# Seven plain pairs, token forms dealt one step per pair, plain tokens in idle tiles

## The chip, the core and the metric

The kernel runs on one core of a Trainium2 chip. Its engines work side by side, each through its own queue in order: TensorE (PE, with weight loads listed as PEld) multiplies, VectorE (DVE) and ScalarE (ACT) work elementwise, GpSimd (POOL) too, and SyncE (SP) issues most transfers. The metric is the device time of one execution in microseconds; lower is better.

## The reference

A two-layer decoder trunk on 512 tokens of width 1024. Layer 0 mixes tokens with retention and mLSTM heads, layer 1 with sparse attention. After each mixer comes the feed-forward block that this change touches, and then a gated per-layer embedding:

```python
def conv_ffn(h, w_up, conv_w, conv_b, w_down):
    a, b = jnp.split(h @ w_up, 2, axis=-1)
    a = causal_dwconv(a, conv_w, conv_b)
    return (jax.nn.gelu(a) * b) @ w_down

h = h + conv_ffn(rms_norm(h, ffn_norm_g[i]), ffn_w_up[i], ...)
e = rms_norm(p[i] @ ple_w[i], ple_norm_g[i])
gate = jax.nn.sigmoid(rms_norm(h, ple_gate_norm_g[i]) @ ple_w_gate[i])
h = h + gate * e
```

w_up is 1024 x 5632, w_down 2816 x 1024, the convolution is causal over three tokens, all in float32.

## The kernel before

**Precision.** Each float32 operand is split into a rounded part (hi) and a remainder (lo); a product is three matmuls, hi x hi, hi x lo and lo x hi (`mm3`, lines 176 to 178). A weight block is loaded into a raw tile `wr`, ACT writes the rounded part `wh` (L136), DVE the remainder `wl` (L137). The pool `wp` has three buffers of each.

**The feed-forward stage** (`ffn`) keeps tokens in columns: h is eight tiles of 128 x 512. `norm_in` makes the plain tokens, hi and lo of each of the eight h tiles times the norm's gain (L244, L245), in 16 of the 22 `g` tiles. The hidden width 2816 is 22 blocks f of 128. Block f needs a pair: a(f) from one half of w_up and b(f) from the other.

- Blocks below `PLAIN` (6) are **plain pairs** (`mm_up`): two products of a 128-row weight block with the tokens, 2 x 8 x 3 matmuls of 512 columns. `act_up` (L1386 to L1389) then scales by the norm (`rb`), convolves (L1374 to L1376), applies gelu (L1377), scales again on POOL (L1388), multiplies by b and keeps hi and lo as `gt[f]` in two g tiles.
- The others are **spread pairs** (`up`): the pair is seen as a 2 x 2 block product and done in seven products instead of eight, each on half the tokens: 4 x 3 matmuls of 256 columns. They need sums of weight blocks (class `Weights`: raw tiles `one` in wr, `two` in an `ep` slot by f modulo 4, and `es`; split parts fh/fl, gh/gl, eh/el, one buffer each) and sums of token halves, the **token forms** (`forms`), four steps of seven y tiles each. ACT copies a bank between two products that share it (L1447).

`down` (a job) multiplies the kept blocks of a part of the hidden width (`PARTS`) with two row blocks of w_down and adds to h (L1479). One job is named in each round of the loop; the first part, three blocks, is named in rounds 3 to 6. `e.early(m)` reads a tile of the embedding back from DRAM, squares it (L232) and adds it up on DVE (L234), one tile in each of rounds 1 to 8, the norm in round 9.

**What sets the order.** The program names instructions in loop order; a planner then gives each engine its sequence ahead of time, from a model of durations, from data dependencies and from free buffers. `high_priority(offset=AHEAD)` lets weight loads and splits go 500 places ahead of their place in the program. `behind(engine)` ties what a block issues on an engine behind the last instruction named there before the block. PSUM has four banks `a`, three `b` and one `o`; a plain pair takes one a and one b, a down job two b.

The round before the change:

```python
if f == 1:
    self.forms(n, C_FFN + 8 * i)
if jobs:
    down(*jobs.pop(0))
e.early(f - 1)
```

Of the kernel before, what the change touches and what calls it, by code (L numbers as in the profile page):

```python
# [11 lines left out]
F32 = mybir.dt.float32  # L12
F32R = mybir.dt.float32r
# [7 lines left out]
P = 128  # L21
T = 512
NTT = T // P
D = 1024
KD = D // P
# [14 lines left out]
UNITS = ((3, (0,)), (3, (1,)), (2, (0,)), (2, (1,)), (1, (0, 1)), (0, (0, 1)))  # L40
BANKS = {"a": 4, "b": 3, "o": 1}
AHEAD = 500
PLAIN = 6
H = T // 2

C_AB, C_NSA, C_FFN, C_PLE, C_PLG = 0, 8, 16, 32, 48
# [17 lines left out]
class Trunk:  # L64
# [73 lines left out]


    def load_late(self, src):  # L140
        raw = self.wp.tile([P, 1024], F32, name=self.nm("wr"), tag="wr")
        hi = self.wp.tile([P, 1024], F32R, name=self.nm("wh"), tag="wh")
        lo = self.wp.tile([P, 1024], F32R, name=self.nm("wl"), tag="wl")
        with self.tc.high_priority(offset=AHEAD):
            self.nc.sync.dma_start(raw, src)
        return (hi, lo), lambda: self.nc.scalar.activation(hi, raw, AF.Copy), lambda: self.nc.gpsimd.tensor_tensor(lo, raw, hi.bitcast(F32), ALU.subtract)

    def load(self, src, n=1024, cuts=1):

        nc = self.nc  # L150
        eng = {"v": nc.vector, "g": nc.gpsimd}[self.lo_seq[0]]
        self.lo_seq = self.lo_seq[1:] + self.lo_seq[0]
        raw = self.wp.tile([P, 1024], F32, name=self.nm("wr"), tag="wr")
        hi = self.wp.tile([P, 1024], F32R, name=self.nm("wh"), tag="wh")
        lo = self.wp.tile([P, 1024], F32R, name=self.nm("wl"), tag="wl")
        with self.tc.high_priority(offset=AHEAD):
            for c in range(cuts):
                s = slice(n // cuts * c, n // cuts * (c + 1))
                nc.sync.dma_start(raw[:, s], src[:, s])
                self.split(hi[:, s], lo[:, s], raw[:, s], eng)  # L160
        return hi, lo

    def load_parts(self, srcs, n):
        raw = self.wp.tile([P, 1024], F32, name=self.nm("wr"), tag="wr")
        hi = self.wp.tile([P, 1024], F32R, name=self.nm("wh"), tag="wh")
        lo = self.wp.tile([P, 1024], F32R, name=self.nm("wl"), tag="wl")
        w = slice(0, n * len(srcs))
        with self.tc.high_priority(offset=AHEAD):
            for x, src in enumerate(srcs):
                self.nc.sync.dma_start(raw[:, x * n : x * n + n], src)  # L170
            self.split(hi[:, w], lo[:, w], raw[:, w])
        return hi, lo
# [5 lines left out]
        mm(out, al, bh, start=False, stop=last, **kw)  # L178

    def packed(self, src):  # L180
        raw = self.wp.tile([P, 1024], F32, name=self.nm("wr"), tag="wr")
        w = self.wp.tile([P, 1024], F32R, name=self.nm("wh"), tag="wh").rearrange("p (k c m) -> p k c m", k=KD, c=2)
        r = raw[:, : KD * 64].rearrange("p (k m) -> p k m", k=KD)
        with self.tc.high_priority(offset=AHEAD):
            self.nc.sync.dma_start(raw[:, : KD * 64], src)
            self.split(w[:, :, 0], w[:, :, 1], r)
        return w
# [66 lines left out]

    def forms(self, n, c0):
        nc = self.nc
        minus = self.sc()
        nc.scalar.activation(minus, n.b, AF.Copy, scale=-1.0)
        sub = lambda out, a, b: nc.vector.tensor_tensor(out, a, b, ALU.subtract)
        neither = lambda out, a, b: nc.vector.scalar_tensor_tensor(out, a, -1.0, b, ALU.mult, ALU.subtract)  # L260
        n.f = []
        for k in range(KD // 2):
            x1, x2 = self.sc(), self.sc()
            for x, kk in ((x1, k), (x2, k + KD // 2)):
                nc.vector.scalar_tensor_tensor(x, self.h[kk], self.col(c0 + kk), minus, ALU.mult, ALU.mult)
            ta, tb = self.sc(), self.sc()
            b11, b12, b21, b22 = x1[:, :H], x1[:, H:], x2[:, :H], x2[:, H:]
            sub(ta[:, :H], b11, b12)
            neither(ta[:, H:], b22, ta[:, :H])
            sub(tb[:, :H], b22, b12)  # L270
            neither(tb[:, H:], b21, ta[:, H:])
            one = self.y()
            self.split(one[:, :H], one[:, H:], b11, nc.gpsimd)
            got = {1: (one[:, :H], one[:, H:])}
            for src, left, right in ((x2, 2, 3), (ta, 5, 6), (tb, 7, 4)):
                hi, lo = self.y(), self.y()
                self.split(hi, lo, src, nc.gpsimd if left == 2 else nc.vector)
                got[left], got[right] = (hi[:, :H], lo[:, :H]), (hi[:, H:], lo[:, H:])
            n.f.append(got)

    def norm_scale(self, n):
        self.norm_sum(n)
        self.norm_cast(n)
# [1069 lines left out]
    def ffn(self, i, e):  # L1353
        nc, I, tc = self.nc, self.I, self.tc
        with ExitStack() as ctx:
            fp = ctx.enter_context(tc.tile_pool(name=f"ffn{i}", bufs=1))

            def g_tile():
                return fp.tile([P, T], F32R, name=self.nm("g"), tag="g", bufs=22)

            n = self.norm_in(C_FFN + 8 * i, g_tile)
            gt = {}

            def mm_up(f):
                self.cycle = ("a", "b")
                return self.ws(I["w_up"][i, f], n), self.ws(I["w_up"][i, NF + f], n)
# [13 lines left out]
            def keep(f, c):  # L1380
                gt[f] = g_tile(), g_tile()
                self.split(*gt[f], c)
# [9 lines left out]
            class Weights:  # L1392
# [8 lines left out]

                def load(me):
                    f = me.f
                    me.one = self.wp.tile([P, 1024], F32, name=self.nm("wr"), tag="wr")
                    me.two = self.slot(f % 4).rearrange("p a t -> p (a t)")
                    nc.sync.dma_start(me.one, I["w_up"][i, f])
                    nc.sync.dma_start(me.two, I["w_up"][i, NF + f])
                    nc.gpsimd.dma_start(me.two[:, :T], me.two[:, T:], accum_op=ALU.add)  # L1408
# [14 lines left out]

            ahead = [Weights(PLAIN)]

# [10 lines left out]

            def product(ps, w, name, first):
                hi, lo = w[name]
                for k in range(KD // 2):
                    s = slice(k * P, k * P + P)  # L1440
                    self.mm3(ps, hi[:, s], lo[:, s], *n.f[k][name], first and k == 0, k == KD // 2 - 1, skip_group_check=True)

            def up(f):
                w = weights(f)
# [23 lines left out]
            def down(part, j):  # L1468
                f0, f1 = PARTS[part]
                w = (f1 - f0) * P  # L1470
                hi, lo = self.load_parts([I["w_down"][i, m, :, f0 * P : f1 * P] for m in (2 * j, 2 * j + 1)], w)
                self.cycle = ("b",)
                for b in range(2):
                    m = 2 * j + b
                    ps = self.bank()
                    for f in range(f0, f1):
                        s = slice(b * w + (f - f0) * P, b * w + (f - f0 + 1) * P)
                        self.mm3(ps, hi[:, s], lo[:, s], gt[f][0], gt[f][1], f == f0, f == f1 - 1)
                    nc.vector.tensor_tensor(self.h[m], self.h[m], ps, ALU.add)  # L1479

            self.lo_seq = "v"
            first = mm_up(0)
# [3 lines left out]
            for f in range(1, NF):  # L1486
                if f < PLAIN:
                    if f == PLAIN - 1:
                        with tc.high_priority(offset=AHEAD):
                            ahead[0].load()  # L1490
                            ahead[0].open()
                    act_up(f, *mm_up(f))
                else:
                    up(f)
                if f == 1:
                    self.forms(n, C_FFN + 8 * i)
                if jobs:
                    down(*jobs.pop(0))
                e.early(f - 1)
                for part, (f0, f1) in enumerate(PARTS):  # L1500
                    if f == f1 - 1:
                        jobs += [(part, j) for j in range(KD // 2)]
# [6 lines left out]
    class Embed:  # L1509
# [4 lines left out]
        def step(self, m):  # L1514
            if m == 0:
                self.inputs()
            if m % 4 == 0:
                self.w = self.k.load(self.k.I["w_ple"][self.i, m // 4])
            self.keep(m, self.products(m, self.w))
# [25 lines left out]

        def early(self, m):
            tr = self.k
            if m < KD:
                t = tr.sc()
                tr.nc.sync.dma_start(t, self.away[m * P : (m + 1) * P])  # L1550
                tr.acc_square(self.n, m, t, tr.nc.vector)
            elif m == KD:
                tr.norm_scale(self.n)
# [144 lines left out]
```

## Time and profile before

| | |
|---|---|
| time, median of 3 runs | 1365.17 us (1364.6 to 1366.2) |
| time of the profiled execution | 1365.49 us |
| its span | 1363.5 us |
| PE busy | 1338.6 us, 98% |
| DVE busy | 1007.2 us, 74% |
| ACT busy | 733.2 us, 54% |
| POOL busy | 415.3 us, 30% |
| mean granted PE clock | 0.994 |

The page cuts the span into 40 slices of 34 us and gives each engine's share of busy time in tenths. "The windows" give busy time and number of instructions for chosen stretches, with the granted clock of PE (1 is full), the DMA share and GB/s. A group's row gives line, engine, operation, tiles written and read, shape, count, busy us and mean ns, and after the second bar the idle time before it and what ended it. A row of the timeline gives start, duration, engine, line and tiles; brackets hold the idle time before it. A row of waits gives who waited for whom, us in total, times, and the longest.

### The profile page before, as it was taken

How to read it: one execution, taken by the hardware profiler on the slowest of the kernel's cores; microseconds unless marked ns; L12 is line 12 of the kernel's file. 1: busy time of each engine (PE TensorE's matmuls, PEld its weight loads, DVE VectorE, ACT ScalarE, POOL GpSimd, SP SyncE). 2: the span in 40 equal slices, each digit the busy share in tenths (PEclk: the TensorE clock that was granted, in tenths of full speed). 3: DMA queues.
4: the chain of work that ended last, by engine and by line, in shares of the span. 5: the costliest groups of instructions: out<-in, count | busy, mean ns of one | idle time of the engine just before them, and what ended most of it. 6: DMA issues, size and time to landing. Idle time of an engine off the chain costs nothing.

```text
span 1363.5 us, 21238 instructions
## 1 busy us (share of the span) xinstructions
PE 1338.6 (98%) x7854; PEld 1155.8 (85%) x7854; DVE 1007.2 (74%) x1644; ACT 733.2 (54%) x1313; POOL 415.3 (30%) x424
## 2 busy tenths in 40 slices
PE   9999999989999999999999999999989999999998
PEld 6888888768999999988788888887868999999987
DVE  5765866797777767687777878766797777767675
ACT  5357525454455445455366888674454455445452
POOL 3356422241111110330421887573240111110320
PEclk9999999989999999999999999999999999999999
DMA  6522348233555553423243331124233555553431
GB/s 221 157 99 93 109 139 247 89 105 109 156 160 153 166 140 101 155 97 116 95 156 110 105 94 51 32 82 126 80 101 116 158 154 158 158 146 95 155 101 70
DMA packets 69456, 168.82 MB, mean 124 GB/s; under 512 B 8164, under 2 KB 12900, under 8 KB 69352
## 3 DMA queue, kind: packets, MB, share of 16 engines
q1 hardware_dynamic: 59848, 150.55, 33.5%
q0 software_dynamic: 9216, 16.78, 7.5%
q8 instruction: 62, 1.02, 0.3%
q14 instruction: 42, 0.34, 0.1%
q10 hardware_dynamic: 288, 0.14, 0.0%
HBM read 147.76 MB, written 7.35 MB: 114 GB/s over the span
## 4 chain that ended last, share of the span: by engine, by line
PE 82%; DVE 9%; ACT 3%; issue 2%; DMA 2%; POOL 1%; SPq 0%; POOLq 0%; DVEq 0%; ACTq 0%
PE ps L176 23%; PE ps L177 23%; PE ps L178 23%; PE ps L1108 3%; PE ps L1083 2%; DVE wl L137 2%; PE ps L1052 1%; PE ps L1053 1%; ACT wh L136 1%; PE ps L432 1%; DVE sc L1376 1%; PE ps L1054 1%; POOL acc L234 1%; DMA emb<-ep 1%; PE ps L978 1%
## 5 line engine op out<-in xcount | busy, mean ns | idle before, releaser
L136 ACT ACTIVATE wh<-wr 128x1024 fp32r<-128x1024 f32 (+2 forms) x184 | 188.8, 1028 | 187.7 <-PE ps L177 109.0
L137 DVE TENSOR_TENSOR wl<-wr,wh 128x1024 fp32r<-128x1024 f32 (+2 forms) x167 | 211.1, 1265 | 53.5 <-ACT wh L136 51.8
L176 PE MATMUL ps<-y,wh 128*128 128x512 f32 (+1 forms) x664 | 230.1, 350 | 1.0 <-ACT y L136 1.0
L177 PE MATMUL ps<-y,wh 128*128 128x512 f32 (+1 forms) x664 | 229.4, 347 | 0.1
L178 PE MATMUL ps<-y,wl 128*128 128x512 f32 (+1 forms) x664 | 228.2, 347 | 0.3 <-DVE wl L137 0.3
L176 PE MATMUL ps<-g,wh 128*128 128x512 f32 x544 | 213.4, 397 | 8.2 <-ACT wh L136 3.9
L178 PE MATMUL ps<-g,wl 128*128 128x512 f32 x544 | 215.0, 395 | 3.8 <-DVE wl L137 3.7
L177 PE MATMUL ps<-g,wh 128*128 128x512 f32 x544 | 215.1, 395 | 0.1
L176 PEld LDWEIGHTS ps<-y,wh 128*128 128x128 f32 x664 | 125.7, 189 | 19.0 <-ACT y L136 1.4
L177 PEld LDWEIGHTS ps<-y,wh 128*128 128x128 f32 x664 | 125.6, 189 | 16.5 <-DVE y L137 0.6
L178 PEld LDWEIGHTS ps<-y,wl 128*128 128x128 f32 x664 | 125.5, 189 | 16.1 <-DVE wl L137 0.7
L176 PEld LDWEIGHTS ps<-g,wh 128*128 128x128 f32 x544 | 103.7, 191 | 30.2 <-DVE hp L1479 5.3
L178 PEld LDWEIGHTS ps<-g,wl 128*128 128x128 f32 x544 | 103.4, 190 | 27.0 <-DVE wl L137 6.3
L177 PEld LDWEIGHTS ps<-g,wh 128*128 128x128 f32 x544 | 103.7, 191 | 21.6 <-DVE g L245 1.6
L1415 POOL DMA_DIRECT2D es<-in_w_up_dram x32 | 28.0, 892 | 235.6 <-DMA es<-in_w_up_dram 112.2
L1447 ACT ACTIVATE sc<-ps 128x256 f32<-128x256 f32 x128 | 47.7, 373 | 87.6 <-PE ps L178 87.5
L1408 POOL DMA_DIRECT2D ep<-ep x32 | 27.4, 856 | 212.1 <-DMA ep<-in_w_up_dram 73.2
L1068 POOL TENSOR_SCALAR pr<-pr,sm,gate 128x512 f32<-128x512 f32 (+3 forms) x128 | 76.8, 624 | 29.2 <-DVE sm L1066 25.3
L234 POOL TENSOR_TENSOR acc<-acc,sc 128x512 f32<-128x512 f32 x36 | 57.4, 1594 | 90.7 <-ACT sc L232 89.3
L1479 DVE TENSOR_TENSOR hp<-hp,ps 128x512 f32<-128x512 f32 x96 | 64.2, 681 | 23.3 <-PE ps L178 22.9
L137 DVE TENSOR_TENSOR el<-es,eh 128x512 fp32r<-128x512 f32 x32 | 22.1, 691 | 79.6 <-ACT eh L136 79.5
L1057 ACT ACTIVATE pr<-ps,nmx 128x512 f32<-128x512 f32 (+3 forms) x128 | 67.7, 536 | 12.7 <-DVE nmx L1055 6.8
(338 smaller groups left out, 3354.3 us busy)
## 6 DMA issues: line engine op xcount, KB each, us to landing
wr<-in_w_up_dram SPq DMA_DIRECT2D x56, 512.0 KB, 3.7
ep<-in_w_up_dram SPq DMA_DIRECT2D x32, 512.0 KB, 4.5
wr<-in_w_down_dram SPq DMA_DIRECT2D x64, 256.0 KB, 4.8
es<-in_w_up_dram SPq DMA_DIRECT2D x32, 256.0 KB, 2.6
es<-in_w_up_dram POOLq DMA_DIRECT2D x32, 256.0 KB, 5.8
ep<-ep POOLq DMA_DIRECT2D x32, 256.0 KB, 3.3
wr<-in_w_plg_dram SPq DMA_DIRECT2D x16, 512.0 KB, 3.6
wr<-in_w_down_dram SPq DMA_DIRECT2D x32, 192.0 KB, 2.5
```

What stands on the lines that cost most here:

```text
L136: self.nc.scalar.activation(hi, src, AF.Copy)
L137: (eng or self.nc.vector).tensor_tensor(lo, src, hi.bitcast(F32), ALU.subtract)
L176: mm(out, ah, bh, start=first, stop=False, **kw)
L177: mm(out, ah, bl, start=False, stop=False, **kw)
L178: mm(out, al, bh, start=False, stop=last, **kw)
L234: eng.tensor_tensor(n.acc, n.acc, sq, ALU.add)
L1057: nc.scalar.activation(pr[:, b], s[:, b], AF.Exp, bias=nmx[:, b : b + 1], accum_out=sm[:, bs[b] : bs[b] + 1])
L1068: nc.gpsimd.tensor_scalar(prs[b], prs[b], sm[:, b : b + 1], gate[:, j, hd, 1 + b : 2 + b], ALU.mult, ALU.mult)
L1108: nc.tensor.matmul(po[0:m, cols], vv[i][:, b, g, 0:m], src, start=False, stop=last and b == 1 and i == 0 and part == 0)
L1415: nc.gpsimd.dma_start(me.s3, I["w_up"][i, me.f][:, :T], accum_op=ALU.add)
L1447: copy = lambda out, ps: nc.scalar.activation(out, ps, AF.Copy)
L1479: nc.vector.tensor_tensor(self.h[m], self.h[m], ps, ALU.add)
```

## The change

`PLAIN` is 7: block 6 becomes a plain pair. The token forms are four closures, one run in each of rounds 1 to 4. `early` moves from rounds 1 to 9 to rounds 8 to 16. The plain tokens 0 to 3 lie in the tiles fh, fl, gh, gl (hi in one half, lo in the other), 4 to 6 in ep slots 0 to 2, and token 7 in two g tiles, of which there are 20 instead of 22. The raw tile wr has four buffers instead of three, in all stages. Each spread product and each down product's matmuls are tied behind the PE instruction named before it.

```diff
-PLAIN = 6
+PLAIN = 7
...
-        raw = self.wp.tile([P, 1024], F32, name=self.nm("wr"), tag="wr")
+        raw = self.wp.tile([P, 1024], F32, name=self.nm("wr"), tag="wr", bufs=4)
...
     def forms(self, n, c0):
         nc = self.nc
+        n.f = []
         minus = self.sc()
...
-        n.f = []
-        for k in range(KD // 2):
+
+        def step(k):
             x1, x2 = self.sc(), self.sc()
...
             n.f.append(got)
+
+        return [lambda k=k: step(k) for k in range(KD // 2)]
...
             def g_tile():
-                return fp.tile([P, T], F32R, name=self.nm("g"), tag="g", bufs=22)
-
-            n = self.norm_in(C_FFN + 8 * i, g_tile)
+                return fp.tile([P, T], F32R, name=self.nm("g"), tag="g", bufs=20)
+
+            def x_tiles():
+                for t in ("fh", "fl", "gh", "gl"):
+                    x = fp.tile([P, 1024], F32R, name=self.nm(t), tag=t)
+                    yield x[:, :T]
+                    yield x[:, T:]
+                for k in range(3):
+                    x = self.slot((PLAIN + 1 + k) % 4, F32R)
+                    yield x[:, 0]
+                    yield x[:, 1]
+                while True:
+                    yield g_tile()
+
+            n = self.norm_in(C_FFN + 8 * i, x_tiles().__next__)
...
             def product(ps, w, name, first):
                 hi, lo = w[name]
-                for k in range(KD // 2):
-                    s = slice(k * P, k * P + P)
-                    self.mm3(ps, hi[:, s], lo[:, s], *n.f[k][name], ...)
+                with self.behind(nc.tensor):
+                    for k in range(KD // 2):
+                        s = slice(k * P, k * P + P)
+                        self.mm3(ps, hi[:, s], lo[:, s], *n.f[k][name], ...)
...
                     ps = self.bank()
-                    for f in range(f0, f1):
-                        s = slice(...)
-                        self.mm3(ps, hi[:, s], lo[:, s], gt[f][0], gt[f][1], ...)
+                    with self.behind(nc.tensor):
+                        for f in range(f0, f1):
+                            s = slice(...)
+                            self.mm3(ps, hi[:, s], lo[:, s], gt[f][0], gt[f][1], ...)
...
                 if f == 1:
-                    self.forms(n, C_FFN + 8 * i)
+                    forms = self.forms(n, C_FFN + 8 * i)
+                if forms:
+                    forms.pop(0)()
                 if jobs:
                     down(*jobs.pop(0))
-                e.early(f - 1)
+                e.early(f - PLAIN - 1)
...
         def early(self, m):
             tr = self.k
-            if m < KD:
+            if 0 <= m < KD:
```

More of the change, by code (lines that the diff above doesn't have):

```diff
@@ L152, in load @@
         self.lo_seq = self.lo_seq[1:] + self.lo_seq[0]
-        raw = self.wp.tile([P, 1024], F32, name=self.nm("wr"), tag="wr")
+        raw = self.wp.tile([P, 1024], F32, name=self.nm("wr"), tag="wr", bufs=4)
         hi = self.wp.tile([P, 1024], F32R, name=self.nm("wh"), tag="wh")
@@ L163, in load_parts @@
     def load_parts(self, srcs, n):
-        raw = self.wp.tile([P, 1024], F32, name=self.nm("wr"), tag="wr")
+        raw = self.wp.tile([P, 1024], F32, name=self.nm("wr"), tag="wr", bufs=4)
         hi = self.wp.tile([P, 1024], F32R, name=self.nm("wh"), tag="wh")
@@ L180, in packed @@
     def packed(self, src):
-        raw = self.wp.tile([P, 1024], F32, name=self.nm("wr"), tag="wr")
+        raw = self.wp.tile([P, 1024], F32, name=self.nm("wr"), tag="wr", bufs=4)
         w = self.wp.tile([P, 1024], F32R, name=self.nm("wh"), tag="wh").rearrange("p (k c m) -> p k c m", k=KD, c=2)
@@ L1403, in load @@
                     f = me.f
-                    me.one = self.wp.tile([P, 1024], F32, name=self.nm("wr"), tag="wr")
+                    me.one = self.wp.tile([P, 1024], F32, name=self.nm("wr"), tag="wr", bufs=4)
                     me.two = self.slot(f % 4).rearrange("p a t -> p (a t)")
@@ L1438, in product @@
                 hi, lo = w[name]
-                for k in range(KD // 2):
-                    s = slice(k * P, k * P + P)
-                    self.mm3(ps, hi[:, s], lo[:, s], *n.f[k][name], first and k == 0, k == KD // 2 - 1, skip_group_check=True)
+                with self.behind(nc.tensor):
+                    for k in range(KD // 2):
+                        s = slice(k * P, k * P + P)
+                        self.mm3(ps, hi[:, s], lo[:, s], *n.f[k][name], first and k == 0, k == KD // 2 - 1, skip_group_check=True)
             def up(f):
@@ L1475, in down @@
                     ps = self.bank()
-                    for f in range(f0, f1):
-                        s = slice(b * w + (f - f0) * P, b * w + (f - f0 + 1) * P)
-                        self.mm3(ps, hi[:, s], lo[:, s], gt[f][0], gt[f][1], f == f0, f == f1 - 1)
+                    with self.behind(nc.tensor):
+                        for f in range(f0, f1):
+                            s = slice(b * w + (f - f0) * P, b * w + (f - f0 + 1) * P)
+                            self.mm3(ps, hi[:, s], lo[:, s], gt[f][0], gt[f][1], f == f0, f == f1 - 1)
                     nc.vector.tensor_tensor(self.h[m], self.h[m], ps, ALU.add)
```

## The prediction

> **What bounds the kernel now.** I read the page first, then the waits of TensorE (PE), then two stretches in windows, then single rows.
>
> ```profile
> PE 1338.6 (98%) x7854; PEld 1155.8 (85%) x7854; DVE 1007.2 (74%) x1644; ACT 733.2 (54%) x1313; POOL 415.3 (30%) x424
> PE   9999999989999999999999999999989999999998
> PEclk9999999989999999999999999999999999999999
> PE 82%; DVE 9%; ACT 3%; issue 2%; DMA 2%; POOL 1%; SPq 0%; POOLq 0%; DVEq 0%; ACTq 0%
> ```
>
> PE is busy for 98% of the span and holds 82% of the chain that ended last. Two slices dip, number 9 and number 30: one in each layer's feed-forward stage. VectorE's (DVE's) 9% of the chain asks where DVE holds PE up. The waits of PE say it:
>
> ```profile
> PE ps L176 <- ACT wh L136: 5.1, 3, 2.0
> PE ps L178 <- DVE wl L137: 4.0, 5, 1.5
> PE ps L176 <- DVE hp L1479: 3.9, 2, 2.2
> ...
> PE ps L176 <- ACT sc L1447: 1.0, 2, 0.6
> ```
>
> Split weights (wh, wl) come late, and a DVE add (L1479) frees a PSUM bank late. Only 1.0 us hangs on the copies between products of the spread stage (L1447). The windows place it: two over all engines from the first plain pair's activation to the first spread product, two over the second half of those, then a long steady stretch.
>
> ```profile
> core 0: us, PE busy (x) PEld busy (x) DVE busy (x) ACT busy (x) POOL busy (x), PEclk, DMA share, GB/s
> 256.00:317.00 61.00, 55.56 (x229) 43.94 (x228) 54.87 (x76) 31.00 (x48) 22.73 (x14) 0.94 0.30 95
> 284.00:317.00 33.00, 27.56 (x106) 20.75 (x105) 30.30 (x43) 15.56 (x24) 11.45 (x7) 0.90 0.39 119
> 969.00:1032.00 63.00, 56.83 (x235) 45.12 (x234) 54.77 (x75) 31.72 (x48) 22.88 (x14) 0.95 0.31 96
> 998.00:1032.00 34.00, 27.83 (x105) 21.11 (x104) 30.25 (x43) 15.29 (x24) 11.66 (x8) 0.90 0.39 123
> 331.00:600.00 269.00, 268.36 (x1800) 248.06 (x1799) 197.91 (x298) 134.06 (x207) 39.71 (x37) 1.00 0.49 140
> ```
>
> To turn counts into time I need the pace. Matmuls overlap, so the pace is start to start, not the 0.39 us that a row gives as duration:
>
> ```profile
> 289.69 0.39 PE L176 MATMUL ps<-g,wh 128*128 128x512 f32 x1
> 290.37 0.39 PE L176 MATMUL ps<-g,wh 128*128 128x512 f32 x1
> ...
> 296.94 0.39 PE L178 MATMUL ps<-g,wl 128*128 128x512 f32 x1
> 299.28 0.63 PE L176 MATMUL ps<-g,wh 128*128 128x512 f32 x1 [1.95 <-ACT wh L136]
> 301.51 0.80 PE L178 MATMUL ps<-g,wl 128*128 128x512 f32 x1 [1.17 <-DVE wl L137]
> ...
> 329.11 0.28 PE L176 MATMUL ps<-y,fh 128*128 128x256 f32 x1
> 330.43 0.28 PE L178 MATMUL ps<-y,fl 128*128 128x256 f32 x1
> ```
>
> Between 289.69 and 290.37 lie three matmuls of 512 columns: 0.2267 us each. Between 329.11 and 330.43 lie eleven intervals of 256 columns: 0.12 us each.
>
> Now the loss. 284 to 317 holds 106 matmuls of 512 columns: 106 x 0.2267 = 24.0 of 33 us, so **9.0 us are lost**. 998 to 1032: 105 x 0.2267 = 23.8 of 34, **10.2 us lost**. Of each, a tenth of the stretch (granted clock 0.90), 3.3 to 3.4 us, is lost to the clock; the rest to the gaps. In 331 to 600 PE is busy for 268.36 of 269 us: the spread stage has nothing to give.
>
> Why there? From 256 to 317 DVE has 54.87 us of work while PE needs 229 x 0.2267 = 51.9 us: DVE is short by 3.0 us before any latency counts. The other layer: 54.77 against 235 x 0.2267 = 53.3. DVE's groups, 256 to 331:
>
> ```profile
> L137 DVE TENSOR_TENSOR wl<-wr,wh 128x1024 fp32r<-128x1024 f32 x9 | 12.8, 1419 | 4.6 <-ACT wh L136 4.6
> L265 DVE SCALAR_TENSOR_TENSOR sc<-hp,cols,sc 128x512 f32<-128x512 f32 x8 | 6.2, 800 | 0.0
> L1376 DVE SCALAR_TENSOR_TENSOR sc<-a,cols,sc 128x510 f32<-128x510 f32 x6 | 6.0, 993 | 0.0
> L137 DVE TENSOR_TENSOR y<-sc,y 128x512 fp32r<-128x512 f32 x8 | 5.3, 678 | 0.0
> L1375 DVE SCALAR_TENSOR_TENSOR sc<-a,cols,sc 128x511 f32<-128x511 f32 x6 | 4.7, 786 | 2.2 <-ACT sc L1374 2.2
> L1386 DVE TENSOR_TENSOR a<-ps,rb 128x512 f32<-128x512 f32 x6 | 4.1, 683 | 2.1 <-PE ps L178 2.1
> L137 DVE TENSOR_TENSOR g<-sc,g 128x512 fp32r<-128x512 f32 x6 | 4.1, 682 | 0.0
> L1389 DVE TENSOR_TENSOR sc<-ps,sc 128x512 f32<-128x512 f32 x6 | 4.1, 680 | 1.4 <-PE ps L178 1.4
> L1479 DVE TENSOR_TENSOR hp<-hp,ps 128x512 f32<-128x512 f32 x6 | 3.9, 675 | 0.0
> L137 DVE TENSOR_TENSOR wl<-wr,wh 128x768 fp32r<-128x768 f32 x4 | 3.8, 948 | 0.0
> L234 DVE TENSOR_TENSOR acc<-acc,sc 128x512 f32<-128x512 f32 x4 | 3.4, 854 | 2.1 <-ACT sc L232 2.1
> ```
>
> The token forms (L265, L259, L260, y) stand in one clump, all named at f = 1, so the activations of pairs 3 to 5 are pushed behind them. A second cause is memory: 16 of the 22 g tiles hold the plain tokens until pair 5 has been multiplied, so gt[3] to gt[5] find no tile before then.
>
> **The change part by part.**
>
> *Seventh plain pair.* Removed: 7 products x 4 x 3 = 84 matmuls at 0.12 = 10.08 us. Added: 2 x 8 x 3 = 48 at 0.2267 = 10.88 us. Cost 0.8 us of PE in each layer, **+1.6 us**, on the path, because PE is the path. For DVE a pair moves from the spread form to the cheaper plain one.
>
> *Forms dealt, embedding squares later.* No instruction goes; `early` only moves seven pairs back, with its SP loads, ACT squares and DVE adds (L234). In the stage up to the border DVE loses the four L234, 3.4 us. It gains a pair's activation (0.683 + 0.786 + 0.993 + 0.680 + 0.682 = 3.8), two weight splits (2 x 1.419 = 2.8), one down job (0.948 + 2 x 0.675 = 2.3) and the split fl, 1.2 (row below). 54.9 - 3.4 + 3.8 + 2.8 + 2.3 + 1.2 = 61.6 us. PE gains 10.9 for the pair and 18 x 0.2267 = 4.1 for the job: 51.9 + 15.0 = 66.9 us. DVE falls from 106% of PE's time to 92%: **the stage turns from DVE-bound to PE-bound**. That is the step that carries the forecast. The spread stage takes all eight squares: DVE is at 197.91 of 269 there, and at most 8 x 0.854 = 6.8 us fits in its 71 us of slack; on SP's queue the eight loads stand behind weight loads that PE does not wait for.
>
> What stays: in 61 us DVE was idle for 6.1 (chains through ACT and POOL). If all of that came again, 61.6 + 6.1 = 67.7 against 66.9 leaves 0.8 us; in the other layer 54.8 + 6.7 + 8.2 = 69.7 against 53.3 + 15.0 = 68.3 leaves 1.4. Lower end: none, if those idle moments were made by PE's own gaps. Upper end: half of today's loss, 9.6 us in all. I take **+2.2 us** for both layers, because the budget row is the nearer one.
>
> *Plain tokens in idle tiles.* Same instructions, other addresses. It frees g tiles for gt[0] to gt[8], so pairs 3 to 6 can be kept at once. The price: fh, fl, gh, gl now hold tokens 0 to 3 until the last plain pair has read them, and slots 0 to 2 hold tokens 4 to 6. Today the f split was made 80 us ahead:
>
> ```profile
> 235.32 1.06 ACT L136 ACTIVATE fh<-ep 128x1024 fp32r<-128x1024 f32 x1 [3.93 <-DMA ep<-ep]
> 236.42 1.23 DVE L137 TENSOR_TENSOR fl<-ep,fh 128x1024 fp32r<-128x1024 f32 x1 [4.17 <-ACT fh L136]
> ...
> 314.53 0.88 POOL L1408 DMA_DIRECT2D ep<-ep  x1 [6.00 <-DVE wl L137]
> ```
>
> After, token 0 is free seven k-steps before the pair ends (7 x 0.68 = 4.8 us), token 3 four steps (2.7 us). Then come a down job, 4.1 us, and products 1 and 2, 24 x 0.12 = 2.9 us, before the g parts are read and 1.4 us more before the f parts. The four splits take 2 x 1.06 on ACT and 2 x 1.23 on DVE, under 3 us when they go first: **0**, hidden by the job. If that cover were gone, at most those 3 us a layer. Slot 0's load for pair 8 waits for token 4; its accumulate on POOL (0.88 us to issue) holds back POOL's product for pair 6's activation, whose g tile is read only by a later job. Pair 8 begins some 15 us later: 0.
>
> *Fourth raw buffer.* It lets a load start one tile sooner. PE waits for no raw load in the table above, so between 0 and a gain of one weight wait (5.1 + 4.0 us are mostly the stalls already counted): **0**.
>
> ```profile
> L1447 ACT ACTIVATE sc<-ps 128x256 f32<-128x256 f32 x128 | 47.7, 373 | 87.6 <-PE ps L178 87.5
> ```
>
> *Fixed order.* Products and down matmuls of the spread stage go in program order, where today they are shuffled. Each bank copy (L1447) then has one product, 12 x 0.12 = 1.4 us, as cover. Lower end: minus 1.0 us (the L1447 row). Upper end: the longest such wait, 0.6 us, in each of 30 pairs, 18 us. The row nearest is the steady window with 0.64 us lost in 269: **0**.
>
> *Sum.* 1365.5 (the profiled execution, span 1363.5 and 2.0 around it) - 9.0 - 10.2 + 1.6 + 2.2 = 1350.1. That execution is 0.3 above the median of the runs: **1350 us**.
>
> **Two rules of the Trainium skill.** Rows: gaps of 1.95 and 1.17 us came with a granted clock of 0.90. "TensorE: Matmul & The Clock Gate", section "HAM oscillation — how this bites in real kernels", asks only for no idle gap over about 3.4 us. By that rule the gaps here should not have cost clock at all, and a leftover gap would cost its own length; by the rows it can cost up to 3.3 us more, and they decide. Rows: a 1024-wide split averages 1.419 us in this stretch and the unhindered one at 236.42 took 1.23. "SBUF — State Buffer", section "Who interferes with whom", says that a VectorE instruction with two SBUF inputs and a GpSimd instruction that reads SBUF block one another. That speaks against the dealing: POOL's share of the forms (y) is spread, not removed. The sum above keeps it, since it uses the stretched means.
>
> **The rivals.**
>
> *The stall only moves to the border.* The splits of pair 7 queue behind DVE's arrears: activation 3.8, two splits 2.8, two adds 1.35, then 0.68 for an add of the raw parts and 2.5 for fl and gl: 11.1 us, against 4.8 + 4.1 + 2.9 = 11.8 us until they are read. On the edge. If it slips by 2 to 3 us, with half clock after it, 5 us a layer come back: 1348 + 10 = **1358**. For it: single buffers. Against it: weights have priority over activations.
>
> *The jam stays.* DVE's clump is only reshaped, all 19 us come back: 1365.2 + 1.6 = **1367**. For it: 92% is still high. Against it: 5 us of new slack in each layer.
>
> *Fixed order starves PE (slower).* If product 6 waits for the copy of product 1, all that follows waits too. "TensorE: Matmul & The Clock Gate", section "Step-by-step: what each phase is for", says that matmuls keep program order, only weight loads are pulled ahead. At 0.8 us for each of 30 spread pairs, 24 us: 1348 + 24 = **1372**; it decides from 17 / 30 = 0.57 us a pair, about the longest wait seen once. Against it: ACT is at half load (134.06 of 269), and a copy takes 0.373 of its 1.4 us.
>
> **How the numbers follow.** Forecast (1345 to 1355) 0.66; the border stall 0.18; the jam 0.06; the starved order 0.06; a small effect either way from the fourth buffer in the mixers 0.04. A measurement of this kernel tells about 0.2%, 2.7 us. The range takes the forecast and most of the border case: 1345 to 1360. Faster 0.87, same 0.06, slower 0.07.
>
> **What would show it.** Right: PEclk without a dip in slices 9 and 30; no wait over 1 us on wh L136, wl L137 or hp L1479 between the second plain pair and the first spread product; DVE near 92% there; 0.8 us more matmul time a layer; fh and gh within some 8 us after the last plain pair. Wrong: a gap just ahead of the first fh or gh product (border), dips at the old places (jam), or many small waits on L1447 (order).

## The result and the profile after

The changed kernel takes **1353.55 us** (median of 4 runs, 1352.91 to 1354.07) against 1365.68 before: ratio 0.9912, interval 0.9895 to 0.9929. It is 12.1 us faster; 15.7 were forecast, and the time lies in the forecast case (1345 to 1355).

From the page after the change:

```profile
span 1351.2 us, 21065 instructions
PE 1332.2 (99%) x7782; PEld 1152.1 (85%) x7782; DVE 1023.5 (76%) x1630; ACT 736.5 (55%) x1301; POOL 409.6 (30%) x422
PE   9999999999999999999999999999999999999998
PEclk9999999999999999999999999999999999999999
```

Both dips have left the rows of tenths, of PE and of its clock. The windows after (columns as before) show what is left. The plain stage, first activation to first spread product, is 253 to 334 and 962 to 1044:

```profile
253.00:282.00 29.00, 29.00 (x131) 23.79 (x129) 24.82 (x31) 15.81 (x23) 10.66 (x7) 1.00 0.22 68
253.00:334.00 81.00, 79.13 (x343) 64.61 (x342) 71.41 (x91) 40.24 (x57) 20.51 (x15) 0.98 0.31 98
282.00:290.00 8.00, 6.16 (x20) 4.75 (x20) 8.00 (x12) 5.33 (x8) 2.82 (x3) 0.79 0.20 66
992.00:1000.00 8.00, 5.96 (x25) 4.40 (x24) 8.00 (x13) 5.27 (x9) 2.00 (x2) 1.00 0.20 68
962.00:1044.00 82.00, 78.63 (x345) 63.96 (x345) 71.37 (x91) 40.30 (x56) 20.61 (x16) 1.00 0.30 96
334.00:592.00 258.00, 257.32 (x1732) 238.62 (x1731) 199.89 (x292) 135.33 (x204) 42.43 (x40) 1.00 0.55 150
```

By the prediction's pace: 343 x 0.2267 = 77.8 of 81 us, 3.2 lost; 345 x 0.2267 = 78.2 of 82, 3.8 lost. So 7.0 us of loss stay where 19.2 were. Most of it is one gap of 2.1 us in each layer, and in layer 0 the half clock behind it; in layer 1 a weight split that comes late at 1028 takes 1.7 us more. The waits of PE name the gap, and the timelines of PE, POOL and DVE show how it comes about:

```profile
PE ps L177 <- DVE g L137: 3.7, 2, 1.8
...
281.96 0.49 PE L176 MATMUL ps<-g,wh 128*128 128x512 f32 x1
284.30 0.50 PE L177 MATMUL ps<-g,wh 128*128 128x512 f32 x1 [1.84 <-DVE g L137]
```

```profile
274.75 2.20 POOL L137 TENSOR_TENSOR y<-sc,y 128x256 fp32r<-128x256 f32 x1 [5.14 <-ACT y L136]
276.92 1.75 POOL L1403 TENSOR_TENSOR sc<-sc,rb 128x512 f32<-128x512 f32 x1
278.62 1.74 POOL L137 TENSOR_TENSOR y<-sc,y 128x512 fp32r<-128x512 f32 x1
...
277.42 1.78 DVE L137 TENSOR_TENSOR y<-sc,y 128x512 fp32r<-128x512 f32 x1
279.13 1.51 DVE L260 TENSOR_TENSOR sc<-sc 128x256 f32<-128x256 f32 x1
280.56 0.68 DVE L1404 TENSOR_TENSOR sc<-ps,sc 128x512 f32<-128x512 f32 x1
...
283.56 0.68 DVE L137 TENSOR_TENSOR g<-sc,g 128x512 fp32r<-128x512 f32 x1
```

The first down job, tied behind pair 3, reads gt[2]. Its activation's product (L1403) stands on POOL behind a form's split, then L1404 stands on DVE behind a split left from the first form step and a difference of the second, both stretched (1.78 and 1.51 us; the same forms take 0.68 and 0.41 elsewhere). The lo part is done at 284.2, 2.1 us after PE wanted it. In layer 0 half clock follows (0.79 in that window), in layer 1 the same gap leaves the clock at 1.00.

Both stretched instructions run beside a split on POOL, the one at 278.62. Without the 2.2 us of stretch L1404 could have begun when L1403 was done, at 278.7 instead of 280.6; that would be most of the gap. This is an estimate from these rows, and no run tried it. DVE has no pause here in which to catch up. From 261.2 to 284.2 it is busy for 23.00 of 23.00 us (the third busy time of the row):

```profile
261.20:284.20 23.00, 21.26 (x93) 17.09 (x92) 23.00 (x30) 11.98 (x19) 9.76 (x7) 1.00 0.21 63
```

### The profile page after: what moved, and what is told of

Read it like the earlier page. It is cut to its first block, busy times and chain, and to the rows that moved or that the text cites. A ratio compares the mean times of both kernels' runs of the same rounds, so it can differ in the third digit from the quotient of the medians.

```text
span 1351.2 us, 21065 instructions
## 1 busy us (share of the span) xinstructions
PE 1332.2 (99%) x7782; PEld 1152.1 (85%) x7782; DVE 1023.5 (76%) x1630; ACT 736.5 (55%) x1301; POOL 409.6 (30%) x422
## 5 line engine op out<-in xcount | busy, mean ns | idle before, releaser
L137 DVE TENSOR_TENSOR wl<-wr,wh 128x1024 fp32r<-128x1024 f32 (+2 forms) x169 | 214.7, 1271 | 75.1 <-ACT wh L136 73.7
L176 PE MATMUL ps<-y,wh 128*128 128x512 f32 (+1 forms) x648 | 225.0, 351 | 0.9 <-ACT y L136 0.9
L177 PE MATMUL ps<-y,wh 128*128 128x512 f32 (+1 forms) x648 | 225.3, 348 | 0.0
L178 PE MATMUL ps<-y,wl 128*128 128x512 f32 (+1 forms) x648 | 223.9, 348 | 0.0
L177 PE MATMUL ps<-g,wh 128*128 128x512 f32 x380 | 149.0, 392 | 3.7 <-DVE g L137 3.7
L176 PE MATMUL ps<-g,wh 128*128 128x512 f32 x380 | 149.2, 393 | 0.2 <-ACT g L136 0.2
L178 PE MATMUL ps<-g,wl 128*128 128x512 f32 x380 | 148.5, 391 | 0.0
L176 PEld LDWEIGHTS ps<-y,wh 128*128 128x128 f32 x648 | 122.5, 189 | 18.3 <-ACT y L136 1.3
L177 PEld LDWEIGHTS ps<-y,wh 128*128 128x128 f32 x648 | 122.7, 189 | 15.5
L178 PEld LDWEIGHTS ps<-y,wl 128*128 128x128 f32 x648 | 122.6, 189 | 15.4
L177 PEld LDWEIGHTS ps<-g,wh 128*128 128x128 f32 x380 | 71.9, 189 | 18.1 <-DVE g L137 4.3
L176 PEld LDWEIGHTS ps<-g,wh 128*128 128x128 f32 x380 | 71.8, 189 | 15.1 <-ACT g L136 1.0
L178 PEld LDWEIGHTS ps<-g,wl 128*128 128x128 f32 x380 | 71.7, 189 | 15.1
L176 PE MATMUL ps<-y,gh 128*128 128x256 f32 x240 | 68.4, 285 | 0.8 <-ACT sc L1463 0.5
```

The source lines that it names most:

```text
L137: (eng or self.nc.vector).tensor_tensor(lo, src, hi.bitcast(F32), ALU.subtract)
L176: mm(out, ah, bh, start=first, stop=False, **kw)
L177: mm(out, ah, bl, start=False, stop=False, **kw)
```

## The experiments

To compare stages I took, for each matmul, the time from its start to the next start, less the pace of its width (0.2267 us for 512 columns, 0.1195 for 256), and added it up. "Plain" runs from the first plain matmul to the first product with f or g weights, "spread" from there to the last one. Microseconds lost, layer 0 and layer 1, and the median time with the ratio's interval:

| kernel | plain | spread | time | ratio to before |
|---|---|---|---|---|
| before | 10.8, 11.4 | 2.7, 2.5 | 1365.4 to 1365.7 | |
| after | 5.1, 6.7 | 1.4, 1.3 | 1353.55 | 0.9895 to 0.9929 |
| u_forms | 16.7, 17.4 | 1.9, 1.4 | 1376.93 | 1.0067 to 1.0094 |
| u_tiles | 8.4, 5.6 | 0.9, 0.9 | 1351.60 | 0.9888 to 0.9915 |
| u_order | 5.9, 6.3 | 10.9, 10.8 | 1373.78 | 1.0036 to 1.0063 |
| u_plain | 10.4, 12.3 | 4.7, 2.8 | 1362.73 | 0.9972 to 0.9990 |
| b_forms | 10.1, 10.2 | 2.7, 2.7 | 1363.22 | 0.9975 to 0.9993 |
| b_order | 17.7, 16.0 | 1.0, 1.0 | 1372.91 | 1.0042 to 1.0067 |
| b_plain | 9.4, 11.1 | 3.0, 3.2 | 1365.20 | 0.9989 to 1.0007 |
| u_order_early | 7.7, 10.3 | 2.4, 2.4 | 1362.44 | 0.9963 to 0.9985 |
| u_early | 9.0, 10.1 | 2.2, 2.4 | 1362.15 | 0.9966 to 0.9986 |
| u_raw | 5.1, 6.8 | 1.0, 1.0 | 1352.78 | 0.9890 to 0.9917 |
| w_job4 | 7.0, 7.7 | 0.9, 0.9 | 1357.20 | 0.9923 to 0.9948 |
| w_forms2 | 0.1, 1.4 | 6.0, 8.5 | 1355.56 | 0.9915 to 0.9942 |

The losses are those of the one profiled execution, the time is the median. In u_plain and u_tiles that execution took 3.9 and 2.7 us more than the median, in w_job4 1.8 us less.

Names with u undo one part of the changed kernel (u_order_early two), names with b add one part to the kernel before, names with w vary u_tiles.

**u_forms.**

```diff
-                if forms:
+                while forms:
                     forms.pop(0)()
```

> The changed kernel with all four form steps named in round 1 again. Budget theory (DVE's arrears ahead of the border make the stall; dealing the forms and moving the squares cured it): the activations of pairs 2 to 4 fall behind the clump, 5 to 8 us come back, 1358 to 1362 us, gaps on wh, wl or g before the border. Memory theory (the g tiles that the plain tokens held made the stall): the clump does not matter, 1353 to 1355 us.

23 us worse than the changed kernel, 11 worse than before, and above both expected ranges. Up to the border DVE has no more to do than in the changed kernel (68.4 us against 70.3, 91 instructions each), so the total alone does not decide. The clump makes PE wait twice in each layer: for the wl split of the next pair, which DVE makes behind form steps, and for gt[2] in the tied down job. PE's timeline, with two rows of DVE:

```profile
283.45 0.40 PE L177 MATMUL ps<-fh,wh 128*128 128x512 f32 x1
...
287.56 0.41 DVE L261 SCALAR_TENSOR_TENSOR sc<-sc,sc 128x256 f32<-128x256 f32 x1
287.89 1.21 DVE L137 TENSOR_TENSOR wl<-wr,wh 128x1024 fp32r<-128x1024 f32 x1
...
289.16 0.80 PE L178 MATMUL ps<-fh,wl 128*128 128x512 f32 x1 [5.31 <-DVE wl L137]
...
300.33 0.61 PE L176 MATMUL ps<-g,wh 128*128 128x512 f32 x1 [3.74 <-ACT g L136]
```

**u_tiles.** The plain tokens in g tiles again.

```diff
-            n = self.norm_in(C_FFN + 8 * i, x_tiles().__next__)
+            n = self.norm_in(C_FFN + 8 * i, g_tile)     # g: bufs=22, wr: three buffers
```

> The changed kernel with the plain tokens in 16 of 22 g tiles and three raw buffers again (four do not fit beside 22 g tiles). Memory theory: gt[3] to gt[6] find no tile before pair 6 has been multiplied, most of the old stall comes back, 1360 to 1366 us. Budget theory: 1353 to 1356 us.

Nothing comes back: 1351.6 (1350.5 to 1354.3), just below the budget theory's range and not to be told from the changed kernel. The memory theory falls: with dealing, ties and late squares in place, g tiles held by the tokens cost nothing, and holding the f and g weight tiles with tokens costs nothing either.

**u_order.** No ties.

```diff
-                with self.behind(nc.tensor):
-                    for k in range(KD // 2):
+                for k in range(KD // 2):
```

> The changed kernel without the ties that put spread products and down matmuls in program order. Prediction (order worth nothing): 1353 to 1354.5 us. Order theory (the excess of the spread stages fell from 2.9 and 2.8 to 2.1 and 1.4 us because of the order): 1355 to 1356 us. Third: the planner moves the first down job behind pair 4 and the gap of 2.1 us goes, 1351 us or less.

All three expectations missed: 20 us worse. The plain stage stays good; the loss is in the spread stage, 10.9 and 10.8 us. PE's waits, and two of them on the timelines of PE and ACT:

```profile
PE ps L176 <- ACT fh L136: 11.1, 8, 2.4
...
434.39 0.28 PE L178 MATMUL ps<-y,fl 128*128 128x256 f32 x1
434.59 1.06 ACT L136 ACTIVATE fh<-ep 128x1024 fp32r<-128x1024 f32 x1
435.70 0.39 PE L176 MATMUL ps<-y,fh 128*128 128x256 f32 x1 [1.03 <-ACT fh L136]
...
468.04 0.28 PE L178 MATMUL ps<-y,fl 128*128 128x256 f32 x1
469.13 0.63 ACT L232 ACTIVATE sc<-sc 128x512 f32<-128x512 f32 x1 [2.22 <-DMA sc<-emb]
469.67 1.04 ACT L136 ACTIVATE fh<-ep 128x1024 fp32r<-128x1024 f32 x1
470.76 0.58 PE L176 MATMUL ps<-y,fh 128*128 128x256 f32 x1 [2.44 <-ACT fh L136]
```

The free order puts the first two f matmuls of the next pair right behind the last f product of this one, where the single f tile has yet to be written again. The ties forbid that. Six of the eight waits are like the one at 435.70: 1.03 us, the length of the split itself. Only the longest in each layer, 2.44 us, has more: an embedding square waits 2.2 us for its tile from DRAM at the head of ACT's queue, and the f split stands behind it. 3.4 us of half clock begin at 470.8, after that wait.

**u_order_early.** u_order with `e.early(f - 1)`.

> The changed kernel without the ties, and with the embedding squares back in rounds 1 to 9. In u_order PE waited 11 us for the f split on ACT, in rounds where ACT's queue held a square that waited for its embedding tile from DRAM (2.2 us at the longest) ahead of that split. If the moved squares are the cause: those waits go, 1354 to 1360 us. If the free order itself is: 1370 to 1375 us.

The spread stage falls from 10.9 and 10.8 to 2.4 and 2.4 us, the total by 11 us to 1362.4, between the two expected ranges, while the plain stage gives back 2 to 4 us a layer. No wait for fh is left among PE's waits, so the six are gone too in which no square stood ahead of the split. The late squares are needed for the loss, but the square in ACT's queue explains only the longest waits: with early squares the planner no longer puts the f matmuls of the next pair at that place. Why the one plan does and the other does not stays open.

**u_early.** The changed kernel with `e.early(f - 1)`, ties kept.

> The changed kernel with the embedding squares back in rounds 1 to 9, ties kept. As the prediction counts it, VectorE gets 3.4 us back on its hands before the border, at 97% of PE's time: 1 to 3 us a layer, 1355 to 1360 us. Rival, from u_order_early (squares early were 11 us better without the ties): squares early are better here too, 1346 to 1352 us.

8.6 us worse, above the 2 to 6 expected of DVE's 3.4 us a layer. With early squares the ties are worth nothing (1362.15 with them, 1362.44 without), with late ones 20 us. PE stands in front of the first down job:

```profile
281.73 0.39 PE L178 MATMUL ps<-g,wl 128*128 128x512 f32 x1
285.78 0.79 PE L176 MATMUL ps<-g,wh 128*128 128x512 f32 x1 [3.66 <-ACT g L136]
...
285.13 0.68 DVE L234 TENSOR_TENSOR acc<-acc,sc 128x512 f32<-128x512 f32 x1
```

DVE's first add of a square comes at 285.1, after gt[2]'s last input: the squares did not take DVE's time ahead of this gap, they changed the order. L1390 of that activation starts at 276.28 where it starts at 272.22 in the changed kernel, behind a form step. A loaded embedding tile takes one of the six scratch tiles that forms and activations share; that this is the link was not tried.

**u_plain.** `PLAIN = 6`.

> The changed kernel with six plain pairs, all else kept. Price of the pair alone: 1.6 us less matmul time, 1352 us. Budget theory: PE loses 15 us a layer of cover before the border while DVE loses 9, so 3 to 5 us of stall come back in all or per layer: 1354 to 1360 us.

9 us worse although 1.6 us of matmul time go: the stall before the border comes back in both layers, as the budget theory says, and by more than it gave. The executions spread over 7 us (1359.5 to 1366.6), all of them above the changed kernel's. The edit also starts the squares a round earlier, since they follow `PLAIN`; that share was not told apart.

**b_forms, b_order, b_plain.** One part each on the kernel before: the dealing; the ties; `PLAIN = 7`.

> The kernel before with one edit: the four form steps dealt to rounds 1 to 4. If the clump's place is what counts (u_forms lost 23 us to it), the border stall of 19 us falls by half or more: 1350 to 1358 us. If DVE's total up to the border counts (budget theory, 106% of PE's time, not changed by this edit): at least 3 us a layer stay, with half clock, 1357 to 1362 us. If six plain pairs are the limit: 1363 to 1366 us.

> The kernel before with one edit: products and down matmuls tied in program order. Prediction (order worth nothing by itself): 1364 to 1366 us. If the order carries 20 us by itself, as the difference of u_order to the changed kernel would read: 1345 to 1350 us; but the spread stages lose only some 5 us in the kernel before, so 1360 us would be its best by that count. If u_order's loss came from the moved squares: 1362 to 1366 us.

> The kernel before with one edit: seven plain pairs. Budget theory (DVE at some 97% of PE's time up to the border instead of 106%): part of the stall goes, 1358 to 1364 us. If the clump of forms counts and not the total: 1.6 us of matmul time more and the stall as before, 1366 to 1368 us; if the seventh pair's activation queues behind the clump as well, up to 1377 us as in u_forms.

Alone they give 2.3 us, cost 7.4 us, and give nothing. b_forms keeps most of the stall; its time is above the budget theory's range and in the third, which took six pairs for the limit. b_order missed: its spread stage gains 1.6 us a layer, but in the plain stage the two waits of u_forms come (in layer 0 5.32 us for wl, then 3.05 and 1.56 us for the two parts of gt[2]). b_plain lies between its ranges; its stall falls by 1.7 us in all, the price of the pair.

**u_raw.** Three raw buffers, all else as changed.

> The changed kernel with three raw buffers. Prediction: worth nothing, 1352.5 to 1354.5 us. If u_tiles is the faster one because of its three raw buffers and not because of its tiles: 1350.5 to 1352.5 us. If the fourth buffer carries something: 1355 us or more.

1352.8: the fourth buffer does nothing that can be told.

**w_job4 and w_forms2.** Two tries at the gap that is left, on u_tiles.

```diff
-                if jobs:
+                if jobs and f > 3:          # w_job4
...
-                if forms:
+                if f > 1 and forms:         # w_forms2
```

> u_tiles (plain tokens in g tiles, three raw buffers) with the first down job in round 4 instead of 3. Theory: the gap of 2.1 us that is left in each layer is this job waiting for gt[2], which VectorE makes late behind the second form step; half clock follows it. A round later gt[2] is long there: the gap and the half clock go, 3 to 7 us less than u_tiles, 1345 to 1349 us. Rival: the gap only moves to the next wait for VectorE (the arrears are what counts, not the job), 1350 to 1354 us.

> u_tiles with the form steps in rounds 2 to 5 instead of 1 to 4. Same theory: the second form step no longer stands ahead of gt[2], the gap goes, 1346 to 1350 us. Rival: the arrears come back at the border, where steps now meet the splits of the first spread pair, 1352 to 1356 us.

In w_forms2 the last step reads h after the second down job has added to it, so those forms are of other values; the work is the same. Both are slower than u_tiles, by 5.6 and 4.0 us. PE's timelines, w_job4 first:

```profile
302.12 0.39 PE L177 MATMUL ps<-g,wh 128*128 128x512 f32 x1
304.79 0.50 PE L178 MATMUL ps<-g,wl 128*128 128x512 f32 x1 [2.29 <-DVE wl L137]
```

```profile
344.20 0.50 PE L176 MATMUL ps<-g,wh 128*128 128x512 f32 x1 [0.71 <-ACT g L136]
347.34 0.50 PE L177 MATMUL ps<-g,wh 128*128 128x512 f32 x1 [2.64 <-DVE g L137]
```

The old gap goes in each, and a larger one opens 20 and 60 us later, at another thing that PE takes from DVE: a weight split, and the lo part of a gt. In kind the rivals hold, the gap moves with the order; w_job4's time is above its rival's range. No version that beats the changed kernel was found; u_tiles and u_raw, which are simpler, equal it.

## Why the prediction was right, and where it was not

*The place of the gain: right.* Of the 19.2 us lost in the two stretches, 12.2 went. In the table's plain stage, which begins at the first plain matmul, it is 10.4, mostly since the start of layer 1's stage lost 1.5 us more than before. The spread stages add 2.5. The prediction held that they had nothing to give, from PE's busy share; by the time from start to start they lost 5.2 us before, and b_order, with the ties alone, gains 3.2 of them. 10.4 and 2.5 less the pair's 1.6 are 11.3 of the 12.6 us between the two profiled executions; the rest was not looked into.

*The budget step: right in its number, too strong as the cause.* DVE was put at 92% of PE's time, and it came to 71.41 us against 77.8. But the 106% that the step starts from was read up to 317 us, where eight spread matmuls had slipped in ahead of 40 plain ones:

```profile
317.15 0.28 PE L176 MATMUL ps<-y,wh 128*128 128x256 f32 x1
...
317.99 0.28 PE L177 MATMUL ps<-y,wh 128*128 128x256 f32 x1
318.11 0.40 PE L178 MATMUL ps<-g,wl 128*128 128x512 f32 x1
```

Here is the stage of layer 0 from the first activation to the last plain matmul, for before, after, b_plain and u_forms:

```profile
257.20:327.20 70.00, 64.56 (x272) 51.54 (x271) 60.52 (x85) 35.60 (x54) 24.02 (x15) 0.95 0.34 106
255.00:333.80 78.80, 76.93 (x331) 62.70 (x330) 70.32 (x91) 38.68 (x55) 20.31 (x15) 0.98 0.31 99
256.20:339.80 83.60, 78.13 (x335) 62.70 (x334) 70.51 (x98) 41.07 (x60) 25.67 (x16) 0.98 0.35 110
255.80:346.30 90.50, 80.53 (x329) 64.94 (x329) 68.38 (x91) 38.73 (x55) 24.58 (x15) 0.92 0.27 88
```

By pace PE needs 60.4 us before (262 matmuls of 512 columns, 8 of 256), 74.4 in the changed kernel and in u_forms (328), and 75.0 in b_plain (328 and 5). DVE's busy time, the third, goes from 100% of PE's time (103% in layer 1) to 95%, not from 106% to 92%; that the 92% came out, with both of its terms some 10 us too small, is luck. And the share does not carry the forecast: b_plain has 94% and gained only what the pair costs, u_forms has 92% and loses 34 us in the plain stages. u_plain, back at 104% (61.8 of 59.4 us), suggests that the slack is needed. It is not enough: what counts is which DVE instruction the planner puts ahead of the next thing that PE waits for. Taking back the dealing, the ties, the seventh pair or the later squares each costs 9 to 23 us.

*The leftover stall: mis-sized.* 2.2 us were taken, 7.0 stayed, within the bound of 9.6. Idle moments averaged over the stage hid a local peak: two form steps and three activations fall due in the first 29 us, ahead of the first down job, and DVE is busy throughout the last 23 us before gt[2] is done. The stretch beside POOL, which the prediction weighed against the dealing and then left at its mean, falls into this peak. Half clock of 3.4 us after one gap in two adds 1.5.

*Squares: right in direction, wrong as to why.* Against u_early they are worth 3.9 and 3.4 us in the plain stages, near the 3.4 that were counted, and about 1 us in each spread stage. But the nearness is luck: u_early's gap opens before DVE adds its first square, and 10.2 and 6.8 us of half clock follow. Their place in the spread stage was safe only with the ties. The prediction looked for slack on DVE and at the SP queue, and passed over ACT, where the square waits for its tile.

*Fixed order: wrong as a term.* It was put at 0, from the steady window of the kernel before. By itself it costs 7.4 us; its removal from the changed kernel costs 20, or nothing once the squares are early as well. The row was from a kernel whose squares and forms stood elsewhere. The rival of starved PE did not come: the waits on the copies fell to 0.5 us.

*Tiles and fourth buffer: 0, as measured.* My reason for the tiles, that the tokens' hold on g tiles made the jam, falls with u_tiles. The new single-buffer waits at the border came and were covered as worked out: fl is split at 326.22 and gl at 328.02, ahead of the first spread product at 333.8.

*The seventh pair: 1.6 us.* b_plain agrees: the same time as before with 1.7 us less stall.

## What to carry to other kernels

When a helper engine is near 100% of the bounding engine's time in one stage, a total shows that there can be a stall, but not how long it is or where it goes; list what the bounding engine takes from the helper in order of need, and what stands ahead of each in the helper's queue. Price a bundle of order changes as a bundle: here each of the three parts tried alone gave 0 to 2 us or cost 7, and all of them together gave 12. Look for an instruction that waits for a transfer at the head of a queue whose next entry the bounding engine needs. In the changed kernel squares wait at the head of ACT's queue seven times in the spread stage of layer 0, 6.8 us in all, while PE waits for ACT there for 0.5 us; in u_order one such wait cost PE 2.4 us.

## What the runs showed of the hardware

An idle gap of about 2.1 us (1.84 us after a matmul's modelled end) was followed by 3.4 us of half clock in layer 0 of the changed kernel and by none in layer 1 of the same execution: the granted clock was 0.79 in the one window and 1.00 in the other. In w_forms2 gaps of 0.71 and 2.64 us (at 344.20 and 347.34) were followed by none, the clock was 1.00 from 340 to 356. So no fixed price per gap fits.

The rule that the prediction weighed, from the Trainium skill ("TensorE: Matmul & The Clock Gate", section "HAM oscillation — how this bites in real kernels"), asks only for no idle gap over about 3.4 us. The gap of layer 0 was shorter and half clock came behind it, so keeping to the rule is not enough here.

A form step's first difference (L260, both halves from one tile) took 1.50 to 1.52 us in the six of the changed kernel's eight steps in which a 512-wide POOL split was running when it began, and 0.41 us in the other two.
